# Five small edits to the order of work in a hybrid decoder trunk's token mixer: riders, output norms, the last decay, and two norm sums

## The chip, the cores and the metric

The kernel runs on one core of a Trainium2 chip. A core has a matrix engine (TensorE, PE in the profile), a vector engine (VectorE, DVE), a scalar engine (ScalarE, ACT), GpSimd (POOL), and queues that issue DMAs, here nearly all on SyncE (SP). The metric is the device time of one execution in microseconds (us); the times given are medians over runs on one chip.

## What is computed

A one-layer decoder trunk on 2048 tokens of width 1024, in float32:

```python
mod = (c_act @ w_ada[l] + b_ada[l])[:, None, :]
sh1, sc1, g1, sh2, sc2, g2 = jnp.split(mod, 6, axis=-1)
h = rms_norm(x) * (1.0 + sc1) + sh1
x = x + g1 * token_mixer(h, w_in[l], w_gla_up[l], b_gla[l], lb_all[l], head_gain[l], w_out[l], pos)
h = rms_norm(x) * (1.0 + sc2) + sh2
x = x + g2 * conv_ffn(h, w_up[l], conv_w[l], conv_b[l], w_down[l])
...
return rms_norm(x) * final_gain
```

The token mixer is one input projection, three kinds of heads side by side (retention, HGRN2, GLA), and one output projection. HGRN2 and GLA are gated linear recurrences: each key channel has its own decay at each token.

```python
S_t = diag(exp(log_f_t)) S_{t-1} + k_t^T v_t,  o_t = q_t S_t
...
o_h = merge_heads(rms_norm(o_h)) * jax.nn.silu(hg)
```

So each head's output is normalised and multiplied by a gate before the output projection. The second half, `conv_ffn`, is an up-projection, a causal convolution of width 3, a gated product and a down-projection. The change does not touch it.

## The kernel before

**Arithmetic.** A float32 matmul is made of three passes over operands split into a high and a low part (`split3`, lines 291 to 293). A matrix tile is therefore loaded, cast (its high part, ScalarE) and subtracted (its low part, VectorE), or its low part is read back from a copy kept in DRAM.

**Blocks and units.** The tokens go in four blocks of 512 (b = 0 to 3). In each block seven units run in the order h0, g, h1, h2, h3, r0, r1 (`ORDER`): four pairs of HGRN2 heads, the GLA heads (one unit with two outputs), two pairs of retention heads. A unit projects its queries, keys, values and gates with 512-column or 256-column matmuls (the GEMMs), and hands the rest to a *chain*, a Python generator. After a block's units comes the output projection in two halves; its second half (`out_finish`) is worked off after the first unit of the next block.

**The order on TensorE is written by hand.** Instructions go to TensorE in the order in which the program traces them. A small model of time, `Clock`, decides that order: `adv(us)` says how long the matmuls just traced take, and when the model's time passes the due time of something put there with `at`, that is traced in between. A chain yields the gap after which its next step is due. Some groups of small matmuls *ride*: between a soonest and a latest time they wait for a `pick`, which a chain's level step calls at its end, so that they stand next to other small matmuls; at the latest time they are traced by themselves.

**The order on the other engines is a planner's.** It takes what is ready in its own estimate of time, first what has the higher priority: an instruction's place in the program, put forward by the offset of a `high_priority` block (`CHAIN` is 400, `HOT` is 600, weight tiles have 50). A `marked` instruction is remembered, and a `pinned` one is put behind the last marked one on its engine. On each engine instructions run strictly in the order that came out.

**A gated chain** (`gated`, lines 703 to 850) builds the decayed attention inside a block over seven levels, spans of 1, 2, 4 to 64 tokens. Before a level's matmuls the queries and keys of that span must be decayed on VectorE (`faded`, queries at line 725, keys at line 727), and for the first of a step's two levels copied aside by ScalarE before they are decayed further (`ahead`, lines 732 and 734). A step takes two levels, the fourth step the last one alone. The first step is traced `FIRST_GAP` after the chain began, the next ones `PAIR_GAP` apart. The first step also makes the attention's diagonal (`dots`, tile dt in the profile), which a predicated copy reads out of its PSUM bank (tile near, line 800). Each level's results are laid into the attention matrix by VectorE or ScalarE (`laid`). After the last level the decayed keys are transposed on TensorE (tile kT, line 816), then the state update u rides, and then the output o (one for an HGRN unit, two for GLA). ScalarE copies the output out of PSUM (line 842), and `post` (lines 629 to 640) normalises it: a square on ScalarE, a sum, a Newton iteration of nine dependent small VectorE instructions, a multiplication by the result and one by the gate. 21 us (`POST_GAP`) after the last output the chain transposes it (tile oT, line 646). The banks for dots, u, o, kT, oT and the norm sums are the same two (`late_ps`); output tiles o have two buffers. After its third step a chain lets the next one begin (`yield None`).

**Two norms.** `norm1_stat(b + 1)` begins at unit h3 of block b: it loads the next block's input in eight tiles, squares them on ScalarE, adds the squares on VectorE into one accumulator (tile san), and rides the step that sums the accumulator over partitions on TensorE (tile ssn, `rstd`), whose result is broadcast 14 us later. The other norm, of the mixer's result (`out_finish`), fills such an accumulator as the output projection goes (line 390, squares at 389) and sums it 4.0 us after the projection.

**adaLN rows.** `ada` (line 223) makes one row's worth of the modulation by a VectorE custom instruction, pinned, on a tile that a DMA brings.

Of the kernel before, what the change touches and what calls it, by code (L numbers as in the profile page):

```python
# [17 lines left out]
P = 128  # L18
# [26 lines left out]
NRAW = 2  # L45
HOT = 600
CHAIN = 400

M512, M256, MF, ML, MT, MO, MS = 0.227, 0.12, 0.224, 0.5, 0.44, 1.7, 0.85
LEVEL_GAP = (3.2, 4.2)  # L50
POST_GAP = 21.0
LAND = 7.5
FIRST_GAP = 7.6
PAIR_GAP = (5.2, 6.4)
RIDE = (2.4, 7.4), (3.8, 9.0)
STAT_GAP, STAT_LAND, NORM_GAP = 2.4, 3.0, 2.0
# [67 lines left out]
def trunk(ctx, tc, xT, vecs, cvec, cst, rope, msk, wada, win, walow, wgla, wout, wup, wdown, out):  # L124
# [32 lines left out]
    def tmp(name, shape=(P, 512)):  # L157
        return pt.tile(list(shape), F32, tag="te", name=name, bufs=NTE)
# [91 lines left out]
    def marked(op):  # L250

        mark[:] = [op.ins]
# [131 lines left out]
    def sumsq(acc, x, k, name, sl=slice(0, TB), first=None, room=None):  # L384
        if k == 0 if first is None else first:
            S.activation(acc[:, sl], x[:, sl], AF.Square)
        else:
            sq = (room or late)(f"sq{name}{k}")
            S.activation(sq[:, sl], x[:, sl], AF.Square)
            V.tensor_tensor(acc[:, sl], acc[:, sl], sq[:, sl], op=ALU.add)  # L390
# [179 lines left out]
    def norm1_stat(b):  # L570
        acc = new_acc(f"n1_{b}")

        def part(k):
            x = tmp(f"x{b}_{k}")
            nc.sync.dma_start(x[:], xT[b, :, k, :])
            clock.at(STAT_LAND, lambda: sumsq(acc, x, k, f"n1_{b}_"))
        for k in range(KD):
            clock.at(STAT_GAP * k, lambda k=k: part(k))
        bc1[b] = new_bc1(b)
        clock.ride(rstd(acc, f"n1_{b}", bc1[b][:], lambda: done.add(("n1", b)), gap=14.0), 26.0, 30.0)  # L580

    def norm1_h(b):
        clock.until(lambda: ("n1", b) in done)
# [119 lines left out]
    def gated(name, b, ui, pos, kq, q, decay, subs, qk, sel):  # L703
# [16 lines left out]
        def faded(li):  # L720

            s, ev = LEVELS[li], tree[li]
            nn = TB // (2 * s)
            qv = q[:].rearrange("p h (n t s) -> p h n t s", t=2, s=s)[:, :, :, 1, :]
            V.tensor_tensor(qv, qv, ev[:, :, 0:1].unsqueeze(1).to_broadcast([P, 2, nn, s]), op=ALU.mult)
            kv = kq[:].rearrange("p (n t s) -> p n t s", t=2, s=s)[:, :, 0, :]
            marked(V.tensor_tensor(kv, kv, ev[:, :, 1:2].to_broadcast([P, nn, s]), op=ALU.mult))

        def ahead(li):

# [50 lines left out]
        for li in range(0, 8, 2):  # L781
            pss = [lev_ps(f"lv{name}_{li}") for _ in parts]
            pair_ = li < 6
            if li == 0:
                dots = late_ps("dt" + name)
                for c in range(NCH):
                    tiled(dots[:, c * nh:(c + 1) * nh], qk[:, c * P:(c + 1) * P], sel)
            if pair_:
                level(li, True)
                level(li + 1, False)  # L790
            else:
                level(li, False)
            with tc.high_priority(offset=CHAIN):
                faded(li + 1 if pair_ else li)
                if li < 4:
                    ahead(li + 2)
                if li == 0:
                    pairs = dots[:, 0:NCH * nh].rearrange("p (a n) -> p a n", n=len(subs))
                    for i, near in enumerate(nears):
                        V.copy_predicated(near[:], m_all[:, 80:112].unsqueeze(1).to_broadcast([P, 8, 32]),  # L800
                                          pairs[:, :, i:i + 1].to_broadcast([P, 8, 32]))
                laid(li, pair_)
                if pair_:
                    laid(li + 1, False)
                if li < 4:
                    faded(li + 2)
            adv((2 if pair_ else 1) * ML)
            clock.pick()
            if li == 4:
                yield None  # L810
            if pair_:
                yield PAIR_GAP[two]
# [21 lines left out]
        for i, (rows, v, sg) in enumerate(subs):  # L834
            if i:
                yield RIDE[1]
            o = pu.tile([P, NCH, P], F32, tag="o", name=f"o{name}_{i}")
            heads = [(at, i) for at in attns] if two else [(attns[0], hh) for hh in range(2)]
            ps = attn_out(f"{name}_{i}", b, heads, v, q[:, i, :], W)
            adv(MO)  # L840
            with tc.high_priority(offset=CHAIN):
                S.copy(o[:].rearrange("p c e -> p (c e)"), ps[:])
                post(o, sg, f"{name}_{i}")
            os.append(o)
        held[0] -= len(subs)
# [123 lines left out]
    def retention(nm, b, r, pos, a, kk, kc, q, vsg):  # L969
        v, sg = vsg  # L970
        Sst = states[5 + r]
        gc = c_all[:, C_GC + r:C_GC + r + 1]
        qps, kps = lev_ps("qT" + nm), lev_ps("kT" + nm)
        for c in range(NCH):
            T.transpose(qps[:, c * P:(c + 1) * P], a[:, c * P:(c + 1) * P], ident)
        for c in range(NCH):
            T.transpose(kps[:, c * P:(c + 1) * P], kk[:, c, :], ident)
        qn = pu.tile([P, TB], F32, tag="f", name="qn" + nm, bufs=3)
        with tc.high_priority(offset=CHAIN):
            S.copy(kc[:], kps[:])  # L980
            S.copy(q[:, 0, :], qps[:])
            S.activation(qn[:], qps[:], AF.Copy, scale=gc)
        ps = late_ps("u" + nm)
        for c in range(NCH):
            tiled(ps[:, c * 64:c * 64 + 64], kk[:, c, :], lambda g: v[:, c, g // 64 * 64:g // 64 * 64 + 64])
        with tc.high_priority(offset=CHAIN):
            W = carry(b, Sst, ps, lambda c: gc)
        adv(2 * MT + ML)
        yield 3.5
        yield from room(1)  # L990
        at = pa.tile([P, 8 * P], F32, tag="a4k", name="at" + nm)
        pss = [lev_ps(f"sc{nm}_{hh}") for hh in range(2)]
        for c in range(NCH):
            for g in range(0, P, 32):
                for ps, r0 in zip(pss, (0, 64)):
                    T.matmul(ps[g:g + 32, c * P:(c + 1) * P], kc[r0:r0 + 64, c * P + g:c * P + g + 32],
                             q[r0:r0 + 64, 0, c * P:(c + 1) * P], start=True, stop=True)
        with tc.high_priority(offset=CHAIN):
            for hh, ps in enumerate(pss):
                V.tensor_tensor(at[:].rearrange("p (c h n) -> p c h n", c=NCH, h=2)[:, :, hh, :],  # L1000
                                ps[:].rearrange("p (c n) -> p c n", n=P),
                                causal.unsqueeze(1).to_broadcast([P, NCH, P]), op=ALU.mult)
        adv(MS)
        yield 3.0
        ps = attn_out(nm, b, [(at, hh) for hh in range(2)], v, qn, W)
        o = pu.tile([P, NCH, P], F32, tag="o", name="o" + nm)
        qd = c_all[:, C_QD + 2 * r:C_QD + 2 * r + 2]
        with tc.high_priority(offset=CHAIN):
            V.tensor_tensor(o[:].rearrange("p c (h e) -> p c h e", e=64),
                            ps[:].rearrange("p (c h e) -> p c h e", h=2, e=64),  # L1010
                            qd.unsqueeze(1).unsqueeze(3).to_broadcast([P, NCH, 2, 64]), op=ALU.mult)
            post(o, sg, nm)
        held[0] -= 1
        adv(MO)
        yield None
        yield POST_GAP
        yield from room(1)
        transposed(b, pos, o, nm)
        adv(MT)
# [92 lines left out]
    def out_finish(b, after_pieces=None, begun=(), own=None):  # L1112


        acc = new_acc(f"n2_{b}")
        out_half(b, 1, acc, after_pieces, begun, own)
        rows = list(x1)
        bc = px.tile([P, TB], F32, tag="bc2", name=f"bc2_{b}", bufs=1)

        def part(m):  # L1120
            nc.sync.dma_start(x1d[b, m][:], rows[m])
            t = rows[m] if b == NB - 1 else tmp(f"t2_{b}_{m}")[:]
            V.scalar_tensor_tensor(t, rows[m], SC2[:, m:m + 1], bc[:], op0=ALU.mult, op1=ALU.mult)
            S.activation(t, t, AF.Identity, bias=SH2[:, m:m + 1])
            nc.sync.dma_start(h2d[b, m][:], t)
            if m == KD - 1:
                done.add(("n2", b))

        def then():
            if b == NB - 1:  # L1130
                with tc.high_priority(offset=-100):
                    for m in range(KD):
                        part(m)
                return
            for m in range(KD):
                clock.at(NORM_GAP * m, lambda m=m: part(m))
        clock.at(4.0, rstd(acc, f"n2_{b}", bc[:], then if b else lambda: put_off.append(then), gap=8.0 if b < NB - 1 else 10.0))


    nth = {"w4": 0}  # L1140
# [653 lines left out]
```

## Time and profile before

| | us |
|---|---|
| Median of 3 runs | 2428.83 |
| Lowest and highest | 2428.18 and 2430.6 |
| The profiled execution, its own time | 2435.79 |
| The profiled execution, span of its trace | 2433.8 |

The mean granted TensorE clock of the profiled execution is 0.995 of full speed. In the profile a tile is named without its numbers, and its last letter tells the unit: kTh is the key transposes of an HGRN unit, og an output of the GLA unit, oTr the transposed output of a retention unit. `L816` is line 816 of the kernel. "<-DVE kh L727" behind an idle time says that the engine sat until VectorE had finished an instruction of line 727 that wrote tile kh. A row of a timeline gives the start, the duration, the engine, the line, the operation, what is written and read, the shape and the count, and in brackets the idle time before it. A row of a waits list gives the total, the number of times and the longest.

The mixer runs up to about 1150 us, the MLP from there on. TensorE is busy in 97% of the span, VectorE in 75%, ScalarE in 53%.

### The profile page before, as it was taken

The page shows a single profiled execution, that of the slowest core. Times are in us where ns is not written, and L with a number is a line of the kernel's source. Part 1 is how long each engine was busy: PE and PEld are TensorE (multiplying, and loading weights), DVE is VectorE, ACT ScalarE, POOL GpSimd, SP SyncE. Part 2 cuts the span into 40 slices and gives each one's busy share as a digit, 9 for nine tenths or more (in the row PEclk, how much of TensorE's full clock was granted, in tenths as well). Part 3 has the DMA queues.
Part 4 walks back from the last instruction along what each step waited for, and adds up shares of the span by engine and source line. Part 5 has one row for each costly group of instructions (what it writes and reads, how often), then busy time and mean ns, then how long its engine had stood idle before and what let it go on. Part 6 is the DMA issues. An engine that isn't in the chain of part 4 may idle for free.

```text
span 2433.8 us, 51912 instructions
## 1 busy us (share of the span) xinstructions
PE 2372.3 (97%) x20523; PEld 1967.2 (81%) x20523; DVE 1815.2 (75%) x3391; ACT 1293.1 (53%) x2311; POOL 154.6 (6%) x275
## 2 busy tenths in 40 slices
PE   7999999999999999999999999999999999999998
PEld 5788878788788888878788888888778888888887
DVE  7687856868577746767888888966788787778666
ACT  4765456744666347644654554554444545545452
POOL 1000100000000100001000000000011010000000
PEclk9999999999999999999999999999999999999999
DMA  7655676797687857778554544686665444548663
GB/s 274 211 199 204 224 251 230 260 321 263 238 313 273 296 191 273 255 272 281 186 166 153 168 149 139 213 288 227 217 203 176 148 148 135 153 149 271 214 195 118
DMA packets 228884, 525.78 MB, mean 216 GB/s; under 512 B 25848, under 2 KB 28832, under 8 KB 228640
## 3 DMA queue, kind: packets, MB, share of 16 engines
q1 hardware_dynamic: 225440, 511.98, 62.8%
q0 software_dynamic: 3200, 10.49, 1.2%
q8 instruction: 161, 2.64, 0.4%
q14 instruction: 83, 0.68, 0.1%
HBM read 392.87 MB, written 129.50 MB: 215 GB/s over the span
## 4 chain that ended last, share of the span: by engine, by line
PE 74%; DVE 11%; DMA 7%; ACT 4%; issue 2%; SPq 0%; DVEq 0%; POOL 0%; ACTq 0%
PE X L291 6%; PE X L293 6%; PE X L292 6%; PE Z L292 3%; PE Z L293 3%; PE Z L291 3%; PE dX L292 3%; PE dX L293 3%; PE dX L291 3%; PE psqkvgr L291 3%; PE psqkvgr L292 2%; PE psqkvgr L293 2%; DMA wada<-wada 2%; PE Y L291 2%; PE Y L293 2%
## 5 line engine op out<-in xcount | busy, mean ns | idle before, releaser
L291 PE MATMUL X<-B,A 128*128 128x512 f32 x572 | 222.9, 390 | 1.2 <-ACT u L1470 1.2
L292 PE MATMUL X<-B,A 128*128 128x512 f32 x572 | 222.8, 389 | 0.8 <-DVE B L1167 0.8
L293 PE MATMUL X<-B,A 128*128 128x512 f32 x572 | 222.6, 389 | 0.0
L1167 DVE TENSOR_TENSOR dA<-rd,dA 128x512 fp32r<-128x512 f32 x154 | 106.2, 690 | 92.5 <-ACT dA L1166 92.1
L1166 ACT CAST dA<-rd 128x512 fp32r<-128x512 f32 x154 | 95.5, 621 | 143.1 <-PE dX L293 56.9
L292 PE MATMUL dX<-dB,dA 128*128 128x512 f32 x396 | 154.2, 389 | 3.2 <-DVE dB L1167 3.2
L291 PE MATMUL dX<-dB,dA 128*128 128x512 f32 x396 | 154.1, 389 | 0.5 <-DVE y L1652 0.5
L293 PE MATMUL dX<-dB,dA 128*128 128x512 f32 x396 | 154.1, 389 | 0.0
L1167 DVE TENSOR_TENSOR A<-s,A 128x512 fp32r<-128x512 f32 x176 | 120.6, 686 | 40.8 <-ACT A L1166 40.7
L1166 ACT CAST A<-s 128x512 fp32r<-128x512 f32 x176 | 108.5, 617 | 64.0 <-PE Z L293 40.3
L291 PE MATMUL psvgh<-hvgh,ha 128*128 128x256 f32 x480 | 139.8, 291 | 0.0
L293 PE MATMUL psvgh<-hvgh,ha 128*128 128x256 f32 x480 | 136.4, 284 | 0.0
L292 PE MATMUL psvgh<-lvgh,ha 128*128 128x256 f32 x480 | 136.4, 284 | 0.0
L291 PEld LDWEIGHTS X<-B,A 128*128 128x128 f32 x572 | 107.4, 188 | 23.9 <-ACT u L1470 1.8
L292 PEld LDWEIGHTS X<-B,A 128*128 128x128 f32 x572 | 107.4, 188 | 23.8 <-DVE B L1167 1.6
L293 PEld LDWEIGHTS X<-B,A 128*128 128x128 f32 x572 | 107.4, 188 | 22.3
L291 PE MATMUL Z<-B,A 128*128 128x512 f32 x308 | 120.4, 391 | 1.0 <-ACT B L1166 0.9
L292 PE MATMUL Z<-B,A 128*128 128x512 f32 x308 | 120.3, 391 | 1.0 <-DVE B L1167 1.0
L293 PE MATMUL Z<-B,A 128*128 128x512 f32 x308 | 119.9, 389 | 0.0
L1166 ACT CAST A<-r 128x512 fp32r<-128x512 f32 x132 | 82.1, 623 | 62.9 <-PE Z L293 58.9
L1167 DVE TENSOR_TENSOR A<-r,A 128x512 fp32r<-128x512 f32 x132 | 90.6, 687 | 27.5 <-ACT A L1166 26.3
L1167 DVE TENSOR_TENSOR dB<-rb,dB 128x512 fp32r<-128x512 f32 x154 | 105.6, 688 | 6.2 <-ACT dB L1166 6.1
(488 smaller groups left out, 6796.9 us busy)
## 6 DMA issues: line engine op xcount, KB each, us to landing
gs<-yv SPq DMA_DIRECT2D x154, 256.0 KB, 3.0
rb<-gs SPq DMA_DIRECT2D x154, 256.0 KB, 4.1
r<-wup SPq DMA_DIRECT2D x143, 256.0 KB, 3.5
s<-sumsu SPq DMA_DIRECT2D x132, 256.0 KB, 3.0
wada<-wada SPq DMA_DIRECT2D x48, 512.0 KB, 4.5
rd<-sumsd SPq DMA_DIRECT2D x88, 256.0 KB, 4.1
rd<-wdown SPq DMA_DIRECT2D x66, 256.0 KB, 3.9
x<-xT SPq DMA_DIRECT2D x64, 256.0 KB, 5.2
```

What stands on the lines that cost most here:

```text
L291: T.matmul(ps, lhs[0], rhs[0], start=first, stop=False, skip_group_check=more)
L292: T.matmul(ps, lhs[0], rhs[1], start=False, stop=False, skip_group_check=more)
L293: T.matmul(ps, lhs[1], rhs[0], start=False, stop=last, skip_group_check=more)
L1166: S.copy(hi, src)
L1167: V.tensor_tensor(lo, src, hi, op=ALU.subtract)
```

## The change

```diff
+AFTER = 200
...
-FIRST_GAP = 7.6
+FIRST_GAP = 8.0
...
     def norm1_stat(b):
         acc = new_acc(f"n1_{b}")
 
+        xr, sq = {}, {}
+
         def part(k):
-            x = tmp(f"x{b}_{k}")
-            nc.sync.dma_start(x[:], xT[b, :, k, :])
-            clock.at(STAT_LAND, lambda: sumsq(acc, x, k, f"n1_{b}_"))
-        for k in range(KD):
-            clock.at(STAT_GAP * k, lambda k=k: part(k))
+            if k > 1 and k - 2 in sq:
+                pinned(lambda: V.tensor_tensor(acc[:], acc[:], sq[k - 2][:], op=ALU.add))
+            if 0 < k <= KD:
+                to = acc
+                if k > 1:
+                    to = sq[k - 1] = late(f"sqn1_{b}_{k - 1}")
+                S.activation(to[:], xr[k - 1][:], AF.Square)
+            if k < KD:
+                xr[k] = tmp(f"x{b}_{k}")
+                nc.sync.dma_start(xr[k][:], xT[b, :, k, :])
+        for k in range(KD + 2):
+            clock.at(2.0 * k, lambda k=k: part(k))
         bc1[b] = new_bc1(b)
-        clock.ride(rstd(acc, f"n1_{b}", bc1[b][:], lambda: done.add(("n1", b)), gap=14.0), 26.0, 30.0)
+        clock.ride(rstd(acc, f"n1_{b}", bc1[b][:], lambda: done.add(("n1", b)), gap=14.0), 30.0, 34.0)
...
@@ in faded
-            V.tensor_tensor(qv, qv, ev[:, :, 0:1].unsqueeze(1).to_broadcast([P, 2, nn, s]), op=ALU.mult)
             kv = kq[:].rearrange("p (n t s) -> p n t s", t=2, s=s)[:, :, 0, :]
-            marked(V.tensor_tensor(kv, kv, ev[:, :, 1:2].to_broadcast([P, nn, s]), op=ALU.mult))
+
+            def of_q():
+                return V.tensor_tensor(qv, qv, ev[:, :, 0:1].unsqueeze(1).to_broadcast([P, 2, nn, s]), op=ALU.mult)
+
+            def of_k():
+                return V.tensor_tensor(kv, kv, ev[:, :, 1:2].to_broadcast([P, nn, s]), op=ALU.mult)
+            for op in (of_q, of_k) if li < 6 else (of_k, of_q):
+                done_ = op()
+            marked(done_)
...
@@ in gated
             adv((2 if pair_ else 1) * ML)
-            clock.pick()
+            if li:
+                clock.pick()
...
             with tc.high_priority(offset=CHAIN):
                 S.copy(o[:].rearrange("p c e -> p (c e)"), ps[:])
+            with tc.high_priority(offset=AFTER):
                 post(o, sg, f"{name}_{i}")
...
@@ in retention
+        with tc.high_priority(offset=AFTER):
             post(o, sg, nm)
...
@@ in out_finish
-        clock.at(4.0, rstd(acc, f"n2_{b}", bc[:], then if b else lambda: put_off.append(then), gap=8.0 if b < NB - 1 else 10.0))
+        clock.at(6.0, rstd(acc, f"n2_{b}", bc[:], then if b else lambda: put_off.append(then), gap=8.0 if b < NB - 1 else 10.0))
```

In words: (1) a chain's first step comes 8.0 instead of 7.6 us after its start and no longer picks up riders; (2) the output norms of all units have an offset of 200 instead of 400; (3) at the last level the keys are decayed before the queries, and the mark stands on the queries' instruction; (4) the first norm's loads, squares and adds are staged 2.0 us apart, the adds pinned, and its sums ride 30 to 34 us after its start instead of 26 to 30; (5) the second norm's sums come 6.0 instead of 4.0 us after the output projection. The numbers of instructions and bytes stay as they were.

## The prediction

> **What bounds the kernel now.** I read the page first, then the busy time of two stretches (the token mixer and, from 1190 us, the MLP), then TensorE's waits, then the stretches where its granted clock fell.
>
> ```profile
> span 2433.8 us, 51912 instructions
> ...
> PE 2372.3 (97%) x20523; PEld 1967.2 (81%) x20523; DVE 1815.2 (75%) x3391; ACT 1293.1 (53%) x2311; POOL 154.6 (6%) x275
> ```
>
> ```profile
> 54.00:1150.00 1096.00, 1066.40 (x14558) 889.27 (x14559) 775.19 (x1911) 627.79 (x1275) 52.89 (x97) 0.99 0.73 253
> 1190.00:2400.00 1210.00, 1203.70 (x5400) 993.78 (x5399) 946.65 (x1292) 610.66 (x948) 87.50 (x148) 1.00 0.57 184
> ```
>
> TensorE is the bound: 97% busy, its matmuls in an order written out by hand. The change edits only code of the mixer, where TensorE idles 1096.00 - 1066.40 = 29.6 us; the MLP's 6.3 us are out of its reach. So the question is which of those 29.6 us go, and what comes in their place. In the list of TensorE's waits (total, times, longest):
>
> ```profile
> PE kTh L816 <- DVE kh L727: 7.0, 4, 2.5
> PE oh L150 <- issue: 4.9, 3, 1.8
> ...
> PE ssn L150 <- DVE san L390: 3.7, 3, 1.8
> ...
> PE lvh L751 <- ACT kc L734: 2.3, 2, 1.5
> ...
> PE kTh L816 <- issue: 1.8, 1, 1.8
> ...
> PE ssn L150 <- DVE nearh L800: 1.2, 2, 1.0
> ```
>
> Three of these are named by the diff: the key transposes that wait for the keys' last decay (kTh, 7.0), the norm sums that wait for their accumulator (ssn on san, 3.7), and the norm sums that wait for a PSUM bank still read by the mask copy of a chain's first step (ssn on nearh, 1.2). The idles put down to "issue" (4.9 + 1.8) lie inside groups, no engine released them, and the change has no hold on them.
>
> A wait costs more than itself. In these stretches, the second apart, the granted clock (third figure from the end) is half; they are the only ones of the mixer:
>
> ```profile
> 340.79:344.20 3.41, 3.41 (x10) 2.59 (x8) 1.22 (x8) 0.00 (x0) 0.00 (x0) 0.50 0.95 341
> 347.29:350.70 3.41, 3.41 (x16) 2.81 (x15) 1.60 (x6) 1.95 (x4) 0.00 (x0) 1.00 0.56 177
> 477.32:484.15 6.83, 6.55 (x73) 5.13 (x62) 6.35 (x22) 2.19 (x5) 0.00 (x0) 0.50 0.86 303
> 624.09:627.51 3.42, 3.42 (x10) 2.64 (x9) 1.30 (x8) 0.00 (x0) 0.00 (x0) 0.50 0.06 25
> 723.08:726.49 3.41, 2.92 (x14) 2.95 (x15) 3.31 (x9) 1.79 (x6) 0.00 (x0) 0.50 0.99 327
> 999.56:1002.97 3.41, 3.41 (x14) 3.02 (x13) 3.07 (x8) 2.65 (x6) 0.00 (x0) 0.50 0.79 267
> ```
>
> The second row is a full-rate stretch of the same length: 16 matmuls of 512 columns, a pitch of 0.23 us, against 10 in the first. Half of the busy time at half rate is lost: 1.7 us for each single stretch, 3.3 us for the double one at 477.32. Each begins within 3 us of the start of one of the waits below.
>
> **The norm sums of the output (4.0 to 6.0 us after the out-projection).** The two long ones:
>
> ```profile
> 339.60 0.43 PE L150 MATMUL ssn<-c_all,san 128*32 128x1 f32 x32 [1.81 <-DVE san L390]
> ...
> 623.01 0.43 PE L150 MATMUL ssn<-c_all,san 128*32 128x1 f32 x32 [1.46 <-DVE san L390]
> ```
>
> ```profile
> 337.65 1.28 DVE L223 CUSTOM_DVE_ANT_0 wada<-wada,c_act,vec 128x1024 f32<-128x1024 f32 x1 [3.48 <-DMA wada<-wada]
> ...
> 338.86 0.69 DVE L390 TENSOR_TENSOR san<-san,sqn 128x512 f32<-128x512 f32 x1
> ```
>
> VectorE stands 3.48 us for an adaLN row, and the last add of the sums is behind it, done at 339.55. The new place puts 2.0 us more matmuls of the same projection ahead of the sums, so TensorE comes at about 339.8: the wait of 1.81 just goes, that of 1.46 with 0.5 to spare. With them go the stretches at 340.79 and 624.09, and the third wait of the row, 3.7 - 3.27 = 0.4. The sum: -(1.81 + 1.46 + 0.4) - 2 x 1.7 = **-7.1**. What follows 2 us later, the broadcast and the second norm, has a whole block of projections as cover.
>
> **Keys first, output norms later in line (CHAIN to AFTER).** VectorE before one of the long key waits:
>
> ```profile
> 717.49 0.69 DVE L635 TENSOR_REDUCE omsg<-osqg 128x8 f32<-128x512 f32 x1 [0.87 <-ACT osqg L633]
> ...
> 719.44 0.17 DVE L181 TENSOR_SCALAR orsg<-omsg 128x8 int32<-128x8 int32 x1
> ...
> 721.80 0.68 DVE L725 TENSOR_TENSOR qbh<-qbh,eh 128x512 f32<-128x512 f32 x1
> 722.41 0.68 DVE L639 TENSOR_TENSOR og<-og,orsg 128x512 f32<-128x512 f32 x1
> 723.01 0.42 DVE L727 TENSOR_TENSOR kh<-kh,eh 128x256 f32<-128x256 f32 x1
> ```
>
> ```profile
> 723.57 1.08 PE L816 MATMUL kTh<-c_all,kh 128*128 128x128 f32 x4 [2.53 <-DVE kh L727]
> ...
> 998.50 0.63 PE L816 MATMUL kTh<-c_all,kh 128*128 128x128 f32 x4 [2.53 <-DVE kh L727]
> ```
>
> The key op of 0.42 us stands behind the query op (0.61 to the next start), a multiplication of the GLA head's output norm (0.60), and that norm's serial steps from 719.44 to 721.80 (2.4). Swapping the two decay ops alone gives 0.61 at most in each of the four waits: -2.4. With the output norm behind them too the key comes over 3 us earlier, and all 7.0 go with the stretches at 723.08 and 999.56, (2.92 + 3.41)/2 = 3.2: -10.2. The order on VectorE is the planner's, which I can't read ahead, but the ops that are passed here are just those whose priority falls; I take **-8.0**, nearer to the full end. The output norm has its 21 us until its transposes as cover.
>
> **First steps: 0.4 us later, and no riders.** The worst first step:
>
> ```profile
> 471.01 0.63 ACT L389 ACTIVATE sqn<-x 128x512 f32<-128x512 f32 x1 [2.34 <-DMA x<-xT]
> ```
>
> ```profile
> 475.96 0.46 PE L751 MATMUL lvh<-qc,kc 128*32 128x32 f32 x32 [1.96 <-ACT qc L732]
> ```
>
> ```profile
> x<-xT SPq DMA_DIRECT2D x64, 256.0 KB, 5.2
> ```
>
> ScalarE stood for an input tile of the next block's norm; its later copies came late and the first step with them. The gap of 8.0 takes 0.4 off. The sums no longer ride on this step, which frees the 1.2 of the bank. The restaged norm (8 loads on SP, 8 squares, 7 adds, as many as before) spaces loads by 2.0 instead of 2.4 and squares a tile 2.0 after its load instead of 3.0, against a landing of 5.2: it may help, for loads start earlier, or block ScalarE again. Bounds: -(1.2 + 1.96 + 3.3) = -6.5 if all of it goes, and 3 x (2.34 + 1.7) = +12 if each of three blocks gets such a stall. The nearest row shows a load issued late, which neither spacing cures, so I take **-1.6**. In SP's queue the last load comes 7 x 0.4 = 2.8 us sooner, ahead of weight tiles that it used to follow; no row of TensorE's list waits for a weight's DMA there. The pinned adds queue behind a chain's marked op; only the sums wait for them, now 4 us later.
>
> Riders that lose the first step: in each of four blocks the GLA unit's update and one HGRN unit's, and the norm sums in three, 11 groups. A group alone, and one that rides:
>
> ```profile
> 231.61 0.39 PE L293 MATMUL psqkvgr<-hqkvgr,ha 128*128 128x512 f32 x1
> 231.93 0.65 PE L150 MATMUL uh<-vh,kTh 128*32 128x64 f32 x32
> 232.52 0.50 PE L291 MATMUL psqkvgr<-hqkvgr,ha 128*128 128x512 f32 x1
> 232.85 0.40 PE L292 MATMUL psqkvgr<-lqkvgr,ha 128*128 128x512 f32 x1
> ```
>
> ```profile
> 411.12 0.63 PE L150 MATMUL ug<-vg,kTg 128*32 128x64 f32 x30
> 411.68 0.50 PE L291 MATMUL pshfh<-ha,hhfh 128*128 128x512 f32 x1
> ```
>
> Alone: 232.85 - 231.61 less two full-rate pitches of 0.23 is 0.78; riding: 0.56. So 0.22 each, **+2.4** if all 11 come alone, +1.3 if only half do.
>
> **What becomes late next.** The GLA update is now forced out about 5 us after the first step that it rode on, so its two outputs each ride one step later, and their norms, some 4 us of VectorE each, fall on the next unit's first two steps. The trace has no such order; the nearest row is the wait of second steps for their key copy (2.3 in 2). Bounds: 0, and one of 1.5 with a half-rate stretch in each block, 4 x 3.2 = +12.8. VectorE gets as much work off the steps before, and the levels keep the higher priority, so I take the lower part: two such waits and one stretch, **+4.0**.
>
> **Sum**: -7.1 - 8.0 - 1.6 + 2.4 + 4.0 = -10.3 against the profiled execution (span 2433.8). Its own time was 2435.79, 7.0 over the median of 2428.83; all terms are differences, so 2428.83 - 10.3 = **2418.5**.
>
> **Rivals.** (A) *Slower: the output copy blocks ScalarE.* Output tiles have two buffers, so the HGRN unit's copy after the GLA unit needs the first GLA output transposed.
>
> ```profile
> 453.20 0.60 PE L646 MATMUL oTg<-c_all,og 128*128 128x128 f32 x4
> ```
>
> ```profile
> 460.70 0.58 ACT L842 COPY oh<-oh 128x512 f32<-128x512 f32 x1
> ```
>
> Now there are 7.5 us between. If the GLA outputs come one step, some 6 to 8 us, later, the transposes move to 459 to 461, up to the copy. If ScalarE reaches the copy first, all behind it (level copies, the next first step's queries) waits, at the price of the row at 475.96 with its stretch, 1.96 + 3.3 = 5.3 a block; four blocks: +21.2, against gains of 14.3 net of riders and new waits: **2436**. It decides from three blocks on. Against it: a planner that foresees the transposes puts other ScalarE work first. (B) *The waits move.* The norm's priority shifts nothing and only the swap acts: -7.1 - 2.4 + 2.4 + 4.0 = -3.1, **2425.7**. For it: VectorE is busy throughout these steps. Against: the ops in front of the key. (C) *The half-rate stretches are not due to these waits* and stay, less 3.4 + 2.5 + 1.7 of the terms: gain 10.3 - 3.4 - 2.5 + 1.7 = 6.1, **2422.7**. For it: waits of 1.5 elsewhere drew none; against: all five stand right behind a wait. The Trainium skill, "TensorE: Matmul & The Clock Gate" (section "HAM oscillation — how this bites in real kernels"), lets the clock fall only after idle gaps of over about 3.4 us. By that rule C holds; here 1.46 and 1.81 us sufficed, and the trace decides.
>
> **Chances.** Forecast 0.52, A 0.18, B 0.20, C 0.10. What a measurement of this kernel can tell from no change is about 0.2%, 4.9 us. Faster than that: 0.48 of the forecast, 0.07 of C, 0.04 of B, 0.59. Within it: 0.04 + 0.03 + 0.14 and 0.03 of A, 0.24. Slower: 0.15 of A, 0.02 of B, 0.17. The forecast's own range goes from 2409 (first steps nearly cured, no new waits) to 2427 (the swap alone and waits in two blocks); with A it ends at **2436**.
>
> **What would show it.** Right: no ssn wait near 340 and 623 and full clock there; no key wait over 0.5 us, the key op ahead of the query op and of the output norm; updates alone behind first steps. Wrong: key waits still above 1.5 us; the copy of line 842 as a releaser or long ScalarE idles before it; second steps waiting over 1.5 us with half clock behind them in three or four blocks.

## The result, and the profile after

The changed kernel takes 2416.8 us (median of 4 runs, 2411.75 to 2417.86) against 2429.72 of the kernel before, run beside it (4 runs, 2428.18 to 2435.91). The ratio is 0.9938, with a 95% interval of 0.9915 to 0.9961. The profiled execution of the changed kernel has a span of 2410.0 us and a time of its own of 2411.75, 5 below its median; that of before was 7 above its median. The traces lie 23.8 us apart and the medians only 12.9, so a size read from one trace against the other comes out nearly twice as large as the medians have it.

The head of the page of after:

```profile
span 2410.0 us, 51886 instructions
...
PE 2365.0 (98%) x20523; PEld 1960.7 (81%) x20523; DVE 1817.1 (75%) x3391; ACT 1290.4 (54%) x2311; POOL 154.3 (6%) x275
```

Every engine runs as many instructions as before. Only the page's total, which also counts what no engine is busy with, is 26 lower (51912 before).

The token mixer, from its first matmul to the MLP's first, holds the same 14421 matmuls in both kernels. The windows view gives its length, then the busy time (and instructions) of TensorE, weight load, VectorE, ScalarE and GpSimd, then the granted clock, the DMA share and GB/s. First before:

```profile
53.91:1119.33 1065.42, 1035.82 (x14421) 863.95 (x14422) 753.82 (x1873) 614.24 (x1250) 51.64 (x92) 0.99 0.73 253
```

then after:

```profile
53.90:1098.52 1044.62, 1029.08 (x14421) 858.57 (x14422) 754.84 (x1873) 610.60 (x1250) 51.62 (x92) 1.00 0.74 259
```

Of 20.8 us in the mixer, TensorE's idle time gives 14.1 (1065.42 - 1035.82 = 29.6, down to 15.5), and its busy time the other 6.7. That goes with less time at half rate: 3.4 us of this mixer, 20.5 of the one before (3.41 + 6.83 + 3.42 + 3.41 + 3.41, rows in the prediction). TensorE's waits in after (total, times, longest) show which waits went and which came:

```profile
PE oTg L656 <- ACT oh L860: 3.3, 2, 1.8
PE lvh L768 <- ACT kc L751: 2.5, 2, 1.2
...
PE ssn L151 <- DVE S L694: 2.1, 1, 2.1
...
PE oh L151 <- issue: 1.0, 1, 1.0
...
PE kTh L834 <- DVE sgg L637: 0.9, 1, 0.9
```

Key transposes wait 0.9 us, and no longer for the key; before it was 7.0, and 1.8 more put down to issue. The mixer's norm sums wait for their accumulator nowhere. The idles put down to issue fell from 6.7 to 1.0. The first step near 476 us, which waited 1.96 us for ScalarE's query copy, waits no more. Two of the larger waits are new: the GLA output's transposes behind the output copy of line 860 (842 before), and one wait of norm sums for the last state update of line 694.

That last one is the only wait of the mixer in after behind which the clock fell. TensorE, then VectorE ahead of it, then the stretch:

```profile
201.71 0.59 PE L151 MATMUL ssn<-c_all,san 128*32 128x1 f32 x32 [2.14 <-DVE S L694]
```

```profile
199.89 0.69 DVE L578 TENSOR_TENSOR san<-san,sqn 128x512 f32<-128x512 f32 x1
200.49 0.28 DVE L694 SCALAR_TENSOR_TENSOR Sc<-Sc,eh,uh 128x64 f32<-128x64 f32 x1
200.68 0.69 DVE L578 TENSOR_TENSOR san<-san,sqn 128x512 f32<-128x512 f32 x1
201.29 0.28 DVE L694 SCALAR_TENSOR_TENSOR S<-Sc,eh,uh 128x64 f32<-128x64 f32 x1
```

```profile
202.56:205.97 3.41, 3.41 (x115) 2.69 (x117) 2.47 (x10) 0.49 (x1) 0.00 (x0) 0.50 0.62 206
```

The restaged adds of the first norm stand between the steps of a state update, and the sums come only when both are done. The wait doesn't need the restaging, though: with the old staging put back (last experiment) it is there too. This half-rate stretch is the only one left in the mixer, against five before, one of them double.

### The profile page after: what moved, and what is told of

It reads as the page before. It is cut to its first block, busy times and chain, and to the rows that moved or that the text cites. A ratio compares the mean times of both kernels' runs of the same rounds, so it can differ in the third digit from the quotient of the medians.

```text
span 2410.0 us, 51886 instructions
## 1 busy us (share of the span) xinstructions
PE 2365.0 (98%) x20523; PEld 1960.7 (81%) x20523; DVE 1817.1 (75%) x3391; ACT 1290.4 (54%) x2311; POOL 154.3 (6%) x275
## 4 chain that ended last, share of the span: by engine, by line
PE 77%; DVE 9%; DMA 6%; ACT 4%; issue 3%; SPq 0%; POOL 0%; DVEq 0%; ACTq 0%; POOLq 0%
PE X L292 6%; PE X L293 6%; PE X L294 6%; PE Z L293 3%; PE Z L294 3%; PE Z L292 3%; PE dX L292 3%; PE dX L294 3%; PE dX L293 3%; PE psqkvgr L292 3%; PE psqkvgr L294 2%; PE psqkvgr L293 2%; PE y L292 2%; PE y L293 2%; PE y L294 2%
```

## The experiments

Each ratio is to the kernel before, run beside it on the same chip, with its 95% interval; 0.1% is 2.4 us. Three sets ran on three chips, with medians of before of 2431.53, 2432.89 and 2433.68.

### The parts alone

The norm sums at 6.0 us, in the kernel before:

```diff
-        clock.at(4.0, rstd(acc, f"n2_{b}", ...
+        clock.at(6.0, rstd(acc, f"n2_{b}", ...
```

> The kernel before with one edit: the second norm's sums come 6.0 instead of 4.0 us after the output projection. Theory (a wait takes its half-rate stretch with it): the waits of 1.81 and 1.46 us near 340 and 623 us are gone and the granted clock is full after them; the time falls by 7 us (0.29%). Rival (the half-rate stretches have another cause): the waits are gone, the clock is still half once in each of the two places, and the time falls by 3.5 us. Rival (VectorE comes late anyway, since the adds move too): waits over 1 us stay and the time falls by under 2 us.

Measured: 0.9993 (0.9977 to 1.001), 2431.01 us. In its trace the waits are gone, and the clock stays full where it had fallen; the first fence is from the waits, the second from the windows:

```profile
PE ssn L150 <- DVE san L390: 0.3, 1, 0.3
```

```profile
342.00:345.40 3.40, 3.40 (x44) 2.54 (x45) 0.47 (x2) 0.00 (x0) 0.00 (x0) 1.00 0.93 296
...
621.90:625.30 3.40, 3.40 (x75) 2.60 (x75) 2.58 (x15) 0.29 (x1) 0.00 (x0) 1.00 0.08 29
```

The mechanism holds at the spot, yet the time tells no change: a gain of 7.1 us lies outside the interval, which ends at 5.6. Of the other waits, the issue idles stayed, and the key waits fell from 7.0 to 4.8 with no edit of the keys; the one before 724 us shrank to 0.3 us, the one before 992 us is as long as it was:

```profile
PE oh L150 <- issue: 5.3, 4, 1.8
PE kTh L816 <- DVE kh L727: 4.8, 4, 2.5
```

The output norms at lower priority, in the kernel before (the same in the retention function):

```diff
                 S.copy(o[:].rearrange("p c e -> p (c e)"), ps[:])
+            with tc.high_priority(offset=AFTER):
                 post(o, sg, f"{name}_{i}")
```

> The kernel before with one edit: the output norms' offset is 200 instead of 400. Theory (the norm's ops stand in front of the key's last decay): the key transposes' waits, 7.0 us in 4, fall to under 2 us in all, their two half-rate stretches go, and the time falls by 6 to 9 us. Rival (the planner's order does not depend on it, only the swap of the two decays acts): these waits stay within 1 us of 7.0 and the time within 2 us of before.

Measured: 1.0001 (0.998 to 1.0022). The waits of its trace:

```profile
PE kTh L817 <- DVE orsg L187: 3.3, 2, 1.9
...
PE kTh L817 <- DVE kh L728: 1.1, 1, 1.1
```

Line 187 is a serial step of the output norm. At the place near 727 us VectorE has this order:

```profile
726.59 0.42 DVE L728 TENSOR_TENSOR kh<-kh,eh 128x256 f32<-128x256 f32 x1
...
727.12 0.69 DVE L640 TENSOR_TENSOR og<-og,orsg 128x512 f32<-128x512 f32 x1
```

So the key now passes the norm's two multiplications, but still stands behind its serial steps. The waits for VectorE, 4.4 us, lie between the two forecasts, and the time doesn't move. Alone, the priority buys nothing that shows.

Keys first at the last level (the diff of `faded` alone):

> The kernel before with one edit: at the last level the keys decay ahead of the queries. Theory: each of the key transposes' four waits shrinks by about 0.6 us, the length of the query op, 7.0 to about 4.6 us in all, the half-rate stretches stay, and the time falls by 2 to 3 us. Rival (the swap alone is what cures the waits): they fall under 2 us and the time by 6 us or more.

Measured: 0.9983 (0.9967 to 0.9998), a gain of 4 us whose interval ends just short of nothing. Its waits for the key:

```profile
PE kTh L823 <- DVE kh L731: 1.6, 2, 1.2
```

They fell from 7.0 to 1.6, more than the 2.4 that 0.61 us in each of four waits allowed. So the waits went as the rival said, and the time did not: nearly all of the key waits can go for a gain of about 4 us.

First steps: no riders and the gap of 8.0, in the kernel before:

```diff
-FIRST_GAP = 7.6
+FIRST_GAP = 8.0
...
-            clock.pick()
+            if li:
+                clock.pick()
```

> The kernel before with two edits: no riders on a chain's first step, and that step 8.0 instead of 7.6 us after the chain's start. Theory of the prediction's sum: -1.6 us at the first steps, +2.4 us for groups that come alone, up to +4 us of new waits at second steps: between no change and 5 us slower; the key transposes' waits stay near 7 us. Rival (the GLA outputs come one step later, so their norms no longer stand in front of the key's last decay): the key transposes' waits fall under 2 us by this edit alone and the time falls by 5 us or more.

Measured: 0.9951 (0.9932 to 0.9969), 2417.94 us. The rival came: this part alone has nearly the whole gain. Its key waits are 0.2 for the key and 0.8 for another op, with no edit of the keys or the norms in it:

```profile
PE kTh L817 <- DVE sgg L627: 0.8, 1, 0.8
PE kTh L817 <- DVE kh L727: 0.2, 1, 0.2
```

### Which half of the first step

The second set took the two lines apart (each alone in the kernel before), took both back from the changed kernel, and tried one consequence of the bar by itself. First the gap alone:

> The kernel before with one edit: a chain's first step comes 8.0 instead of 7.6 us after its start. If the two edits of the first step gain through the riders, this one moves nothing by itself: the key transposes' waits stay at 5 us or more and the time within 3 us of before. Rival (0.4 us more for a step's operands is the gain): the waits for ScalarE's query and key copies at first steps go, and the time falls by 5 us or more.

Measured: 1.0051 (1.0032 to 1.007), 2446.25 us, slower, which neither forecast had. Its waits show new places and no common cause:

```profile
PE oh L150 <- issue: 4.4, 3, 2.3
...
PE kTh L816 <- DVE kh L727: 3.4, 1, 3.4
PE uh L150 <- DVE oTh L651: 3.0, 2, 2.0
```

The bar on riders alone:

> The kernel before with one edit: no riders on a chain's first step, the step itself at 7.6 us as before. Theory (the GLA outputs come one step later, so their norms no longer stand in front of the key's last decay): the key transposes' waits fall under 1.5 us and the time falls by 9 to 13 us, all that both edits of the first step gave. Rival (the gap is the gain): these waits stay and the time is within 3 us of before.

Measured: 0.9955 (0.994 to 0.997), 2421.93 us, with 0.5 us of waits of the key transposes for VectorE, as the theory said. Both lines back to 7.6 and riders, in the changed kernel, so that the four other parts remain:

> The changed kernel with the first step as before: riders on it, 7.6 us after the chain's start. Theory: the lower priority of the norms and the swap of the decays must now clear the way of the key by themselves; alone the one gave nothing and the other 2 to 6 us, so the time is 6 to 10 us above the changed kernel, and 2 to 6 us below the kernel before. Rival (the priority and the swap together do what neither does alone): it is within 3 us of the changed kernel.

Measured: 1.0012 (0.9998 to 1.0026), 2434.47 us: without the first step's edit the other four give nothing, though the key waits of this trace are down to 2.0 us. Then, in the kernel before, only the GLA unit's update is held back until 5.0 us after its key transposes, so that it can't ride on it; all other riders stay:

```diff
-        yield RIDE[0]
+        yield (5.0, 7.4) if two else RIDE[0]
```

> The kernel before with one edit: the state update of the GLA unit alone may not ride before 5.0 us after its key transposes (2.4 before), so it misses the next chain's first step and its outputs come one step later; the HGRN updates and the norm sums ride as before. Theory (the GLA outputs' norms are what stood in front of the key): the key transposes' waits at 442, 724 and 998 us go and the time falls by 6 to 12 us. Rival (it is the bank that the other riders hold, or their place, that costs): the key waits stay and the time is within 3 us of before.

Measured: 0.9964 (0.9947 to 0.9981), 2424.46 us. The key waits go, as the theory said:

```profile
PE kTh L816 <- DVE kh L727: 0.2, 1, 0.2
```

Holding back this one group in each block gives 0.36%, and the bar on all riders 0.45%. So most of it is not the emptier first step as such; it is the GLA unit's later update, and what follows from it.

What follows can be read in the third block of the trace. In before the first GLA output rides the second level step, the second output the third:

```profile
698.91 0.46 PE L751 MATMUL lvh<-qbh,kh 128*32 128x32 f32 x30
...
699.22 0.41 PE L150 MATMUL og<-W,qbg 128*32 128x128 f32 x6
...
707.22 0.43 PE L751 MATMUL lvh<-qbh,kh 128*32 128x64 f32 x15
...
707.48 0.42 PE L150 MATMUL og<-W,qbg 128*32 128x128 f32 x7
```

The first output's norm then fills VectorE up to 711.7, and that level's mask copy, for which ScalarE stands, starts only at 712.55. VectorE, then ScalarE:

```profile
711.00 0.69 DVE L640 TENSOR_TENSOR og<-og,sgg 128x512 f32<-128x512 f32 x1
...
712.55 0.30 DVE L763 COPY_PREDICATED nearh<-m_all,lvh 128x128 f32<-128x128 uint32 x1
```

```profile
712.93 1.65 ACT L774 COPY ath<-nearh 32x256 f32<-32x256 f32 x4 [4.37 <-DVE nearh L763]
...
715.70 0.59 ACT L842 COPY og<-og 128x512 f32<-128x512 f32 x1
```

ScalarE stands 4.37 us, the second output's copy comes at 715.70, 6 us after its matmuls, and its norm falls right where the last key op should run (717.49 to 723.01, rows in the prediction). With the bar on riders alone both outputs come one step later, the second behind the 128-column level:

```profile
697.69 0.43 PE L751 MATMUL lvh<-qbh,kh 128*32 128x64 f32 x15
...
697.95 0.41 PE L150 MATMUL og<-W,qbg 128*32 128x128 f32 x7
...
706.02 0.64 PE L751 MATMUL lvh<-qbh,kh 128*32 128x128 f32 x16
706.48 0.40 PE L150 MATMUL og<-W,qbg 128*32 128x128 f32 x8
```

```profile
709.78 0.69 DVE L725 TENSOR_TENSOR qbh<-qbh,eh 128x512 f32<-128x512 f32 x1
710.38 0.42 DVE L727 TENSOR_TENSOR kh<-kh,eh 128x256 f32<-128x256 f32 x1
...
713.38 0.68 DVE L635 TENSOR_REDUCE omsg<-osqg 128x8 f32<-128x512 f32 x1
```

```profile
713.39 0.60 PE L817 MATMUL kTh<-c_all,kh 128*128 128x128 f32 x4
```

Only the first output's norm is ahead of the key now, done by 709.78; the second begins at 713.38, when the key is long through, and TensorE's transposes of it at 713.39 wait for nothing. The query op is still ahead of the key op here, as before the swap: neither the swap nor the priority is needed for it.

The key is not all that the later update moves. In the traces of both kernels (bar alone, held-back update) the first step near 476 us no longer waits for its query copy, and the double half-rate stretch behind that wait is gone, with the gap at 7.6 us as before. The issue idles near 767 and 1042 us (1.60 and 1.45) are gone too. And clearing the key is not enough by itself: the swap alone left 1.6 us of key waits and gained 0.17%, the four parts without the first step's edit left 2.0 and gained nothing. So it is shown that most of the gain comes with the GLA unit's later update; that the key waits are what it consists of is not shown.

### In company

Held-back update, norm sums at 6.0 and keys first together, in the kernel before:

> The kernel before with three edits: the GLA unit's update may not ride before 5.0 us after its key transposes, the second norm's sums come 6.0 us after the output projection, the keys decay first at the last level. It has neither the lower priority of the norms, nor the bar on all riders of a first step, nor the restaged first norm. Theory (these three hold all the gain): 0.55 to 0.75% below before, as the changed kernel or better, with no key wait and no wait of the second norm's sums over 0.5 us. Rival (the parts left out give something in company): 0.3 to 0.45% below before, slower than the changed kernel.

Measured: 0.9957 (0.9944 to 0.9971). The waits went as the theory said, and the time is the rival's. The two add nothing that can be told to the 0.9964 of the first, and whether the parts left out give the rest, the intervals don't say.

The gap back to 7.6, in the changed kernel:

> The changed kernel with the first step at 7.6 us after the chain's start again. Alone the 8.0 cost 0.5%, together with the bar on riders it cost nothing. Theory (it only shifts which groups meet): within 0.15% of the changed kernel, so 0.45 to 0.75% below before. Rival (the 0.4 us are needed or harmful by themselves): waits for ScalarE's key and query copies at level steps rise by 2 us or more and it loses over 0.2%, or it gains over 0.2%.

Measured: 0.9969 (0.9956 to 0.9982), 2426.83 us, half the gain of the whole change (0.9938), though the intervals overlap by a hair (0.9956 and 0.9961). That is more than the theory allowed, and the rival's waits for key and query copies did not rise. Its first wait:

```profile
PE oTh L656 <- DVE S L694: 6.1, 2, 4.0
```

and that of the kernel with both lines back:

```profile
PE ssn L151 <- DVE S L694: 7.1, 3, 4.1
```

The group behind a state update waits for the update's last step, 6.1 and 7.1 us at 7.6, 2.1 in the changed kernel at 8.0. So next to the other edits the longer gap goes with a shorter wait there. With the bar alone beside it, it makes no difference that can be told (0.9951 against 0.9955), and by itself it costs 0.51%; why it does, the runs don't say.

No riders on any step, in the changed kernel:

```diff
-            if li:
-                clock.pick()
```

> The changed kernel with no pick at all: every update, output and norm sum comes alone at its latest time. Theory of the idles put down to issue (TensorE runs out of instructions in a burst of small matmuls, for each stands 2.2 to 2.5 us behind an instruction transfer): with no group next to a level's, these idles fall to zero; some 30 more groups come alone at 0.22 us each, +7 us, and outputs come later. Rival (the idles come by the place in the program, not by bursts): 1 us or more of them stays inside small groups.

Measured: 0.9991 (0.9977 to 1.0005). Barring riders from every step gives up nearly all the gain, so a bar doesn't pay as such. The issue idles did not fall to zero but rose, inside small groups, as the rival said. Its first wait:

```profile
PE og L151 <- issue: 7.4, 3, 3.7
```

The norm's old staging (loads 2.4 apart, squares and adds 3.0 later, the sums still at 30 to 34), in the changed kernel:

> The changed kernel with the first norm's loads, squares and adds as before (2.4 us apart, squares 3.0 us after their load, adds not pinned), its sums still riding 30 to 34 us after its start. Theory (the pinned adds come late): the wait of 2.1 us before the norm sums near 202 us goes with its half-rate stretch, and the time is 1 to 4 us below the changed kernel. Rival (the staging is what keeps ScalarE from standing for an input tile): idles of ScalarE for x tiles rise and the time is 2 us or more above it.

Measured: 0.9948 (0.9931 to 0.9965), 2421.25 us, not to be told from the changed kernel's 0.9938. Neither forecast came. The norm sums still wait 1.87 us for a state update near 202 us, with 3.41 us at half rate from 203.5, so that wait does not need the pinned adds. And ScalarE's idles for input tiles fell (2.2 us against 3.8). The restaging is worth nothing that shows. Nor does any of the twelve kernels beat the changed kernel by more than the intervals.

## Why the prediction was right in the time and wrong in the reasons

**The time.** 2418.5 was forecast, 2416.8 came, in the forecast's own range. The sum of -10.3 against -12.9 hides errors that cancel, so that it came so close is luck. For the norm sums, the key and the output norms -15.1 was forecast; with the restaging they gave +2.9 together without the first step's edit (1.0012, interval -0.5 to +6.3). For the first step's edit, with all that follows from it, +4.8 was forecast; alone it gave -11.9 (0.9951, interval -16.5 to -7.5).

**"What becomes late next", +4.0: the step that failed.** It saw the mechanism (the GLA update is forced out alone, its outputs ride one step later, their norms move) and drew the wrong sign from it: it let the norms fall on the next unit's first steps and priced new waits there, without asking where they stood before. They stood in front of the key. With the outputs one step later the time falls by 0.36% (8.7 us) through the held-back update alone, by 0.45% (10.9 us) through the bar. The waits that the term priced did not come: second steps wait 2.5 us in two places for their key copy in after, 2.3 in two before, with full clock behind. The bounds of this term, 0 to +12.8, left out the side on which it fell.

**"Keys first, output norms later in line", -8.0.** The key waits went as forecast, but not by these edits. The priority alone gives nothing (1.0001) and lets the key pass only the norm's last two instructions; the swap alone gives 0.17%, with an interval from 0.02 to 0.33%; the bar on riders clears the waits without either. The four parts without the first step's edit give nothing (1.0012).

**The norm sums, -7.1.** The waits and the stretches at 340 and 624 went, as forecast, in one trace with this edit alone; the time gives 0.07% with an interval from -0.10 to +0.23%, so at most 5.6 us. The term took two half-rate stretches (3.4) from one execution that was 7 us above its median. Such stretches change from run to run of one kernel. Each run lists its span and its mean granted clock, and (1 - clock) times the span is an estimate of what half rate cost it: the ten runs of this kernel go from 2423.9 us at 0.998 to 2436.7 at 0.993, which is 5 and 17 us of such loss. One trace can't price a stretch, and the sum should have discounted it.

The same estimate, on the means of all runs of a set, splits the gains. Before loses 13.9 us in the set of the bar and 15.0 in that of the swap. The bar alone loses 9.7, so 4.2 of its 10.8 us are clock and 6.6 are other time; the held-back update 10.2, 3.7 of its 8.8. The swap alone loses 10.4, which is all of its 3.7 us and more: the waits that it cleared came back elsewhere. The gap alone loses 21.6, 7.7 of the 13.7 us that it costs.

**First steps, -1.6.** The gap was taken as 0.4 us off a wait. Alone it is +0.51%, 12 us, and its trace has waits in places where before had none: an offset in a hand-written order moves every later step against the other engines, and the term had no row and no bound for that. Beside the other edits the sign turned. The wait of 1.96 us that the term priced did go with its stretch, but it went as well with the bar or the held-back update alone, at a gap of 7.6. The restaging at nothing, inside its bounds, was right in size (0.9948 without it).

**Riders, +2.4.** Not measured by itself. With no riders on any step, the time goes back to 0.9991, which has the sign, but that kernel's 7.4 us at issue are another cost.

**The idles at issue.** The prediction said that the change has no hold on them. They are 6.7 us before and 1.0 after: 5.7 of the 14.1 us of idle time that went in these two traces.

**The rivals.** A's sign came without its mechanism. The copy of line 860 does release the transposes in two places, 3.3 us together. But there the GLA output's second transposes wait for the copy, which reads the bank that they need (`late_ps` has two); the copy waits for no buffer. In the first place it is late because ScalarE stood for an input tile and had level copies to do:

```profile
457.29 0.66 PE L656 MATMUL oTg<-c_all,og 128*128 128x128 f32 x4 [1.78 <-ACT oh L860]
```

```profile
452.41 0.63 ACT L583 ACTIVATE sqn<-x 128x512 f32<-128x512 f32 x1 [1.33 <-DMA x<-xT]
...
456.66 0.58 ACT L860 COPY oh<-oh 128x512 f32<-128x512 f32 x1
```

```profile
457.00:460.40 3.40, 3.11 (x36) 2.78 (x37) 2.19 (x4) 3.40 (x8) 0.00 (x0) 1.00 0.40 152
```

The price forecast for it, 5.3 a block, had a half-rate stretch in it; here the clock stays full. B (only the swap acts) is half right: the priority does nothing, but the waits went all the same, through the first step's edit. C (the stretches are not due to these waits) falls at 340 and 624, where the stretches went with the waits, as far as one trace goes; the stretches elsewhere came and went with the order.

**Readings of the prediction.** That each half-rate stretch begins within 3 us of the start of a wait holds for three of five; at 477.32 and 999.56 it is 3.3 and 3.6 us, and the one at 723.08 begins 0.5 us before its wait ends, not behind it. The sum of A leaves out the +4.0 of new waits, with which it is 2440, and that of B the -1.6 of the first steps.

## What to carry to other kernels

Where a wait names the last of several ops on a busy engine, trace each op in front of it back to where it was issued: moving the group that produces it one step later cleared the waits here, lowering its priority on the engine did not. A wait that is cleared is not yet time gained: the swap cleared most of the key waits for 0.17%. When a change makes something late, ask what it stood in front of before, and let the term's bounds reach below nothing. Gains of half-rate stretches read from one execution are to be discounted, at least by that execution's distance from the median.

## What the runs showed of the hardware

**Idles at "issue" go with fetches of the program.** Over the fourteen traces TensorE has 47 idles of more than 0.7 us put down to issue; every one ends 2.2 to 2.7 us after the start of a transfer of 16 KB on the instruction queue, and 32 of them stand inside or right behind a run of 84 to 131 small matmuls in 2 us. One of before, TensorE first and then the DMA view of a window of 0.3 us shortly ahead of it (packets, MB, share):

```profile
115.01 0.22 PE L150 MATMUL oh<-vh,ath 128*32 128x64 f32 x1
117.04 0.43 PE L150 MATMUL oh<-vh,ath 128*32 128x64 f32 x15 [1.81 <-issue]
```

```profile
q8 instruction: 1, 0.02, 19.5%
```

The matmul at 115.01 and its fellows at 117.04 are of one group, and the profile shows nothing that released them. The mixer of before has 114 such transfers, and four of them stop TensorE for over 0.7 us. That runs of small matmuls use up what has been fetched fits the places; no run took the size of such a run by itself, and in nine traces the idle near 99 us comes behind only eight or nine matmuls in 2 us, so this stays argued. The Trainium skill, "Runtime: NRT & Kernel Launch" (section "Instruction fetch mechanics"), has the fetch in blocks of 16 KiB, mostly hidden. The block agrees with the 0.02 MB of the row. Mostly hidden fits 110 of the 114 transfers; the other four cost 6.6 us in before, and in the kernel with no riders three places at GLA outputs cost 7.4.

**Some short waits are followed by half the clock, others are not.** A wait of 2.14 us was followed by 3.41 us at a granted clock of 0.50 in after, one of 1.78 us by none, in the same execution; in before 1.46 us was enough. What decides it stays open.
